# Twenty columns of experts by pairs instead of sixteen, with a third buffer, splits on GpSimd and separate memory for the last stage

## The chip, the cores and the metric

The kernel runs on one core of a Trainium2 chip. The metric is the device time of one execution in microseconds; of the kernel before there are three runs. A core has five engines with a queue of their own each, and every queue is worked off in order: TensorE (PE: matmuls; PEld: the load of the stationary operand), VectorE (DVE), ScalarE (ACT), GpSimd (POOL) and SyncE (SP). SP and ACT start plain transfers, POOL plain and indexed ones; the transfers themselves run on 16 DMA engines.

## The reference

One encoder layer over 256 tokens of 2048 features. Behind the mixing part (pooling and latent attention) stands PEER, a retrieval over 128 x 128 = 16384 experts of one neuron each:

```python
h = h + jnp.concatenate([y_pool, y_mla], axis=-1) @ w_out[i]
h = h + peer(rms_norm(h, ffn_norm_gain[i]), w_pq[i], sub_k1[i], sub_k2[i], expert_u[i], expert_v[i])
gate = jax.nn.sigmoid(rms_norm(h, ple_norm_gain[i]) @ w_ple_gate[i])
h = h + gate * (p[i] @ w_ple_proj[i])

# in peer: 8 heads pick 16 of 128 x 128 experts for every token, with softmax gates
act = jax.nn.gelu(jnp.einsum('tkd,td->tk', expert_u[ib], xb))
return jnp.einsum('tk,tkd->td', act * gb, expert_v[ib])
```

So each token has 128 expert slots. For a slot the dot product of the token with the expert's row of U is taken, its gelu is multiplied by the gate, and with that coefficient the expert's row of V is added. All of it is in f32.

## The kernel before

**Columns.** The 16384 experts stand as 128 columns of 128. For a dense column the kernel computes all 256 tokens against all 128 experts: the U tile of the column (1 MB) comes in two halves of 128 x 1024, each is split into two fp32r parts (`hi` on ACT, `lo` = value - `hi` on DVE, L108 and L110), and 48 matmuls of 256 columns follow (L220 to L222, three for each of 16 slices). ND = 112 columns go this way, one after the other.

**Pairs.** The other NP = 16 columns (104 to 119) are computed only where a token picked an expert: the pairs (token, expert) are listed in chunks of up to four of one token, 128 chunks to a set, NS = 9 sets (NCH = 8 chunks for a token at most). A *step* takes one of the four pairs of each of 128 chunks and one half of the features: an indexed transfer `ur<-in_UP` brings 128 half rows of U (512 KB), and one DVE instruction (L1106) multiplies them with the tokens' half rows `xr` (512 KB, loaded for every fourth step) and sums. There are 9 x 2 x 4 = 72 steps. After a set its four columns of sums are scattered to `hidD` by indexed transfers (L1119). The `ur` and `xr` buffers are rings of two each; the gather of step k + 2 is issued when step k has been computed.

**The pairs' last stage.** When all sums are in `hidD`, four quarters q of 64 tokens follow (`pair_load_coefs`, `pair_coefs`): POOL loads the sums (L1129) and the gates (L1130) of a quarter into the two `ur` buffers, ACT takes the gelu, DVE multiplies (L1144) and takes the largest magnitude, and POOL writes the coefficients to `coefD` (L1147).

**Groups and lists.** In between, the gates are laid out for the dense columns by small matmuls with one-hot matrices, in 64 *groups* of four tokens (L1015). From the columns that are done, lists of used experts are built in three stages (columns 0 to 79, 80 to 119, 120 to 127: `classes`, `totals`, `ranks`, `places`, then `columns`, L1329 on PE). The list of the first stage names the first 17 tiles of V rows, that of the second needs the pairs' coefficients: its rank matmuls (L1254) wait for them.

**V tiles.** A V tile gathers 128 rows of V (`vraw`, 1 MB, L1382) and their coefficients (`cr`, L1395), splits both, and adds their product. The first eleven stand between the dense columns from column START = 100 on, two halves behind each; the other 86 run at the end, then the gated last matmul.

**What sets the order.** The loop over columns calls `u_hook` twice per column (once more in a V tile). Each call adds to a pace; while it is 1 or more, one task of the queue `side` (selection, groups, lists) is written into the program, and a second pace does the same for the queue `lq` of pair tasks (PAIR_PACE: 0.45 for each call while groups run, 1.0 afterwards). A scheduler then orders PE, ACT, DVE and POOL by times that it estimates; SP keeps the written order. `Feed` (L58 on) loads halves five ahead and splits two ahead; `hi` and `lo` have three buffers each. Splits whose number stands in `on_pool` get their `lo` part on POOL; before, those are two halves of V, none of U.

## Time and profile before

| | |
|---|---|
| median of 3 runs | 1674.48 us (1673.2 to 1678.94) |
| the profiled execution | 1681.48 us, span of its instructions 1679.8 us |
| PE | 1573.0 us busy (94%), 10548 matmuls |
| DVE | 1245.6 us (74%) |
| ACT | 887.8 us (53%) |
| POOL | 470.6 us (28%) |
| DMA | 396.24 MB, mean 236 GB/s |
| mean granted TensorE clock | 0.969 of full speed |

The shares are means over stages with different limits, so the stages are read apart: up to 387 us the layer's first part, then the dense columns to about 1219 us, the rest of the V tiles to 1568 us, and the last matmul. A busy PE counts pipelined matmuls, and one that runs at half clock is as busy as one at full clock; the time of a column is the better measure.

### The profile page before, as it was taken

The page shows a single profiled execution, that of the slowest core. Times are in us where ns is not written, and L with a number is a line of the kernel's source. Part 1 is how long each engine was busy: PE and PEld are TensorE (multiplying, and loading weights), DVE is VectorE, ACT ScalarE, POOL GpSimd, SP SyncE. Part 2 cuts the span into 40 slices and gives each one's busy share as a digit, 9 for nine tenths or more (in the row PEclk, how much of TensorE's full clock was granted, in tenths as well). Part 3 has the DMA queues.
Part 4 walks back from the last instruction along what each step waited for, and adds up shares of the span by engine and source line. Part 5 has one row for each costly group of instructions (what it writes and reads, how often), then busy time and mean ns, then how long its engine had stood idle before and what let it go on. Part 6 is the DMA issues. An engine that isn't in the chain of part 4 may idle for free. (4 is left out here: it accounts for less than half of the span.)

```text
span 1679.8 us, 27995 instructions
## 1 busy us (share of the span) xinstructions
PE 1573.0 (94%) x10548; PEld 1424.9 (85%) x10548; DVE 1245.6 (74%) x2233; ACT 887.8 (53%) x1615; POOL 470.6 (28%) x396
## 2 busy tenths in 40 slices
PE   8999999999999999999899889673989999999997
PEld 6888787999999899999898789663877888888886
DVE  5575658899997688888796779463886667667764
ACT  6765445544543577777533333241456556556653
POOL 0010000000000323232432354431247776676000
PEclk9999999999999999999999999896999999999999
DMA  8663366556555576777799888675778888888263
GB/s 298 206 197 116 126 210 236 178 166 231 182 185 183 184 236 220 254 250 234 259 353 349 316 288 271 240 263 175 227 301 328 297 291 295 287 293 298 84 218 110
DMA packets 101252, 396.24 MB, mean 236 GB/s; under 512 B 14131, under 2 KB 19412, under 8 KB 85620
## 3 DMA queue, kind: packets, MB, share of 16 engines
q1 hardware_dynamic: 59908, 221.26, 39.4%
q0 software_dynamic: 34720, 168.00, 28.7%
q10 hardware_dynamic: 6480, 5.11, 0.9%
q8 instruction: 84, 1.38, 0.3%
q14 instruction: 60, 0.49, 0.1%
HBM read 367.01 MB, written 27.32 MB: 235 GB/s over the span
## 5 line engine op out<-in xcount | busy, mean ns | idle before, releaser
L108 ACT CAST hi<-raw 128x1024 fp32r<-128x1024 f32 (+2 forms) x382 | 392.4, 1029 | 457.6 <-PE bank L221 311.5
L110 DVE TENSOR_TENSOR lo<-raw,hi 128x1024 fp32r<-128x1024 f32 (+2 forms) x382 | 455.7, 1195 | 142.9 <-ACT hi L108 139.4
L222 PE MATMUL bank<-xnH,lo 128*128 128x256 f32 x1792 | 513.8, 288 | 15.7 <-DVE lo L110 15.7
L220 PE MATMUL bank<-xnH,hi 128*128 128x256 f32 x1792 | 520.4, 291 | 1.6 <-ACT hi L108 1.6
L221 PE MATMUL bank<-xnL,hi 128*128 128x256 f32 x1792 | 513.8, 287 | 0.0
L222 PEld LDWEIGHTS bank<-xnH,lo 128*128 128x128 f32 x1792 | 349.2, 196 | 17.2 <-DVE lo L110 16.7
L220 PEld LDWEIGHTS bank<-xnH,hi 128*128 128x128 f32 x1792 | 350.6, 196 | 2.6 <-ACT hi L108 2.0
L221 PEld LDWEIGHTS bank<-xnL,hi 128*128 128x128 f32 x1792 | 350.6, 196 | 0.2
L110 DVE TENSOR_TENSOR lo<-vraw,hi 128x1024 fp32r<-128x1024 f32 x192 | 233.7, 1224 | 104.3 <-ACT hi L108 93.5
L108 ACT CAST hi<-vraw 128x1024 fp32r<-128x1024 f32 x194 | 203.1, 1048 | 103.7 <-PE bank L222 70.2
L221 PE MATMUL bank<-lo,ccH 128*128 128x512 f32 x520 | 208.0, 400 | 2.6 <-DVE lo L110 2.6
L222 PE MATMUL bank<-hi,ccL 128*128 128x512 f32 x520 | 207.2, 398 | 0.0
L220 PE MATMUL bank<-hi,ccH 128*128 128x512 f32 x520 | 156.8, 400 | 23.1 <-ACT hi L108 22.3
L1382 POOL DMA_INDIRECT vraw<-in_V,idx x97 | 129.0, 1330 | 124.2 <-DVE lo L110 49.6
L1099 POOL DMA_INDIRECT ur<-in_UP,uidx x72 | 94.9, 1319 | 243.0 <-DVE hp L1106 183.1
L1395 POOL DMA_INDIRECT cr<-coefD,idx x97 | 126.6, 1305 | 52.9 <-issue 27.2
L220 PEld LDWEIGHTS bank<-hi,ccH 128*128 128x128 f32 x520 | 98.1, 191 | 47.8 <-ACT hi L108 24.5
L221 PEld LDWEIGHTS bank<-lo,ccH 128*128 128x128 f32 x520 | 99.2, 191 | 27.0 <-DVE lo L110 4.1
L222 PEld LDWEIGHTS bank<-hi,ccL 128*128 128x128 f32 x520 | 99.2, 191 | 22.5
L1106 DVE CUSTOM_DVE_ANT_0 ur<-ur,xr 128x1024 f32<-128x1024 f32 x72 | 87.7, 1218 | 36.5 <-DMA ur<-in_UP,uidx 36.4
L233 ACT ACTIVATE oo<-oo,gT 128x128 bf16<-128x128 bf16 x256 | 81.8, 395 | 6.9 <-DVE oo L1004 6.8
L221 PE MATMUL bank<-hgL,hi 128*128 128x256 f32 x256 | 73.3, 287 | 4.0 <-DVE hgL L730 4.0
(401 smaller groups left out, 2380.2 us busy)
## 6 DMA issues: line engine op xcount, KB each, us to landing
raw<-in_U SPq DMA_DIRECT2D x224, 512.0 KB
raw<-in_w_out SPq DMA_DIRECT2D x32, 512.0 KB
raw<-in_w_pq SPq DMA_DIRECT2D x32, 512.0 KB
raw<-in_w_gate SPq DMA_DIRECT2D x32, 512.0 KB
raw<-in_w_in_p SPq DMA_DIRECT2D x16, 512.0 KB
...
```

The costliest lines, as they stand in the source:

```text
L108: self.nc.scalar.copy(hi[:, :w], r)
L110: eng.tensor_tensor(lo[:, :w], r, hi[:, :w].bitcast(F32), op=OP.subtract)
L220: pe.matmul(ps, ah, bh, start=start, stop=False)
L221: pe.matmul(ps, ah, bl, start=False, stop=False)
L222: pe.matmul(ps, al, bh, start=False, stop=stop)
L233: act.activation(dst, ps, AF.Copy, scale=scale)
L1099: pool.indirect_dma_start(out=u, out_offset=None, in_=a["UP"], in_offset=bass.IndirectOffsetOnAxis(ap=lst["uidx"][:, half, s, i:i + 1], ax ...
L1106: tc.keep_in_program_order(dve.tensor_tensor_reduce(out=u, in0=u, in1=lst["x"][s, half], scale=1.0, scalar=0.0, op0=OP.mult, op1=OP.add, a ...
L1382: pool.indirect_dma_start(out=raw, out_offset=None, in_=a["V"], in_offset=bass.IndirectOffsetOnAxis(ap=row(c, i, 0), axis=0))
L1395: pool.indirect_dma_start(out=cr[:, :w], out_offset=None, in_=src, in_offset=bass.IndirectOffsetOnAxis(ap=row(c, i, 1), axis=0))
```

## The change

NP becomes 20: four dense columns fewer (108), four more by pairs. NCH and NS become 10 and 11, which makes 88 steps of the 72. START becomes 96, the pairs' pace while groups run 0.6, the pace of `side` outside the groups 1.3. Rows of U get a third buffer, and `pair_loads(k + 2)` is issued ahead of step k instead of behind it. Of the halves of U tiles 26 to 97 every third has its `lo` part on POOL: `U_POOL` is a range of columns, 144 halves, and a V tile stands among them; POOL gets 49 of the splits. Behind the last step `pair_end` gives the pairs' memory back and opens new memory: two buffers for a quarter's sums, one each for gates and coefficients; between load and use of a quarter stand two empty tasks instead of one (four at the first). One DVE multiplication of the list stage (L1318) goes to ACT. Two empty tasks are put into a list stage, and the loop waits at column START for the first coefficients' loads to be written.

```diff
-NP = 16
+NP = 20
-NCH = 8
-NS = 9
+NCH = 10
+NS = 11
 BETWEEN = 11
-START = 100
-PAIR_PACE = (0.45, 1.0)
+START = 96
+PAIR_PACE = (0.6, 1.0)
+U_POOL = (26, 98)
...
+    first = next(u for u, x in enumerate(units) if x[0] is u_tiles[U_POOL[0]])
+    last = next(u for u, x in enumerate(units) if x[0] is u_tiles[U_POOL[1] - 1])
+    feed.on_pool = [n for n, (u, i) in enumerate(feed.parts) if first <= u <= last and n % 3 == 0]
...
-        u = lp.tile([P, ring_w], F32, name="ur", tag="ur", bufs=2)[:, :1024]
+        u = lp.tile([P, ring_w], F32, name="ur", tag="ur", bufs=3)[:, :1024]
...
         s, half, i = steps[k]
+        if k:
+            pair_loads(k + 2)
         u = lst["u"].pop(k)
...
-        pair_loads(k + 2)
...
+    def pair_end():
         while lst["out"]:
             pair_out()
+        close(cms["L"])
+        cms["L"], st["lp"] = open_pool(name="pairs2", side="right")
+        lst["mx"] = st["lp"].tile([P, NP], F32, name="mx")
+
+    def pair_load_coefs(q):
         lp = st["lp"]
         w = NP * 64
-        hq = lp.tile([P, ring_w], F32, name="ur", tag="ur", bufs=2)[:, :w]
-        gq = lp.tile([P, ring_w], F32, name="ur", tag="ur", bufs=2)[:, :w]
+        hq = lp.tile([P, w], F32, name="hq", tag="hq", bufs=2)
+        gq = lp.tile([P, w], F32, name="gq", tag="gq")
...
-        cq = lp.tile([P, ring_w], F32, name="xr", tag="xr", bufs=2)[:, :NP * 64].rearrange("p (n t) -> p n t", t=64)
+        cq = lp.tile([P, NP, 64], F32, name="cq", tag="cq")
...
+        lq.append(pair_end)
         for q in range(4):
-            lq.extend([lambda q=q: pair_load_coefs(q), lambda: None, lambda q=q: pair_coefs(q)])
+            lq.append(lambda q=q: pair_load_coefs(q))
+            lq.extend([lambda: None] * (4 if q == 0 else 2))
+            lq.append(lambda q=q: pair_coefs(q))
...
-        dve.tensor_scalar(oh[:, 1], oh[:, 0], i2col, None, op0=OP.mult)
+        evac_scaled(oh[:, 1].rearrange("p k n -> p (k n)"), oh[:, 0].rearrange("p k n -> p (k n)"), i2col)
...
-        out = [lambda f=f: f(s) for f in (classes, totals, ranks, places, places2, places3)]
+        out = [lambda f=f: f(s) for f in (classes, nothing, totals, ranks, nothing, places, places2, places3)]
...
-        st["pace"] += 1.75 if st["wk"] and st["groups"] < 64 else 1.0
+        st["pace"] += 1.75 if st["wk"] and st["groups"] < 64 else 1.3
...
+            while j == START and not crs:
+                hook()
```

In the program, the groups stand between columns 23 and 58 (29 and 64 before), the last step of the pairs at column 90 (99), the last list matmul of the first stage in column 94 (99), the first V tile behind column 96 (100), and the rank matmuls of the second stage behind the sixth V tile in both.

POOL's queue where the pairs' steps run beside dense columns; before (a piece of the steps behind the groups; `hidD<-hp` is the scatter of sums):

```order
L1099 DMA ur<-in_UP,uidx 128x1024 x4
L1095 DMA xr<-xnD,rowx 128x1024
L1119 DMA hidD<-hp,hidx 528896x1
L1099 DMA ur<-in_UP,uidx 128x1024 x2
L1119 DMA hidD<-hp,hidx 528896x1
L1099 DMA ur<-in_UP,uidx 128x1024
L1119 DMA hidD<-hp,hidx 528896x1
L1099 DMA ur<-in_UP,uidx 128x1024
```

The same queue now, in the same part (L112 is the split's `lo` half, L1106 the gather of U rows, L1127 the scatter):

```order
L112 TENSOR_TENSOR lo<-raw,hi 128x1024
L1127 DMA hidD<-hp,keys 660992x1
L1106 DMA ur<-in_UP,uidx 128x1024 x2
L1102 DMA xr<-xnD,rowx 128x1024
L112 TENSOR_TENSOR lo<-raw,hi 128x1024
L1106 DMA ur<-in_UP,uidx 128x1024
L1127 DMA hidD<-hp,keys 660992x1
L112 TENSOR_TENSOR lo<-raw,hi 128x1024
L1106 DMA ur<-in_UP,uidx 128x1024 x2
```

Splits of U now stand between gathers and scatters, and each waits until those ahead of it in the queue have been issued.

POOL's queue in the pairs' last stage before, from the loads of quarter 0 to those of quarter 2 (`ur<-hidD` sums, `ur<-gateD` gates, `coefD<-xr` coefficients, `cr` and `vraw` of V tiles):

```order
L1129 DMA ur<-hidD 128x1024
L1130 DMA ur<-gateD 128x1024
L1395 DMA cr<-coefD,idx_11434 128x128
L1382 DMA vraw<-in_V,idx_11434 128x2048
L1147 DMA coefD<-xr 128x8x64 x2
L1129 DMA ur<-hidD 128x1024
L1130 DMA ur<-gateD 128x1024
L1395 DMA cr<-coefD,idx_11434 128x128
L1382 DMA vraw<-in_V,idx_11434 128x2048
L1395 DMA cr<-coefD,idx_11434 128x128
L1147 DMA coefD<-xr 128x8x64 x2
L1129 DMA ur<-hidD 128x1024
```

And now (L1142 loads sums, L1143 gates, L1160 writes coefficients, L1412 and L1399 are those of V tiles):

```order
L1142 DMA hq<-hidD 128x1280
L1143 DMA gq<-gateD 128x1280
L1142 DMA hq<-hidD 128x1280
L1412 DMA cr<-coefD,idx_11115 128x128
L1399 DMA vraw<-in_V,idx_11115 128x2048
L1412 DMA cr<-coefD,idx_11115 128x128
L1160 DMA coefD<-cq 128x8x64 x2
L1160 DMA coefD<-cq 128x4x64
L1143 DMA gq<-gateD 128x1280
L1142 DMA hq<-hidD 128x1280
```

The sums of the next quarter are loaded one quarter ahead; its gates still follow the coefficient writes, of which there are three instead of two.

## Rows read from the trace of the kernel before

**Rows 1.** Busy time of each engine by stretch of the span: from and to (us), length, then busy us and instructions of PE, PEld, DVE, ACT and POOL, the granted TensorE clock, the share of the DMA engines and GB/s.

```profile
387.00:520.00 133.00, 133.00 (x1111) 133.00 (x1110) 125.86 (x303) 62.98 (x79) 3.26 (x6) 1.00 0.61 198
520.00:556.00 36.00, 36.00 (x317) 35.87 (x316) 26.40 (x64) 15.72 (x23) 4.33 (x5) 1.00 0.58 188
556.00:567.00 11.00, 7.51 (x71) 6.89 (x70) 4.05 (x6) 4.00 (x10) 7.54 (x8) 0.96 0.36 113
567.00:818.00 251.00, 251.00 (x2420) 246.93 (x2418) 216.81 (x364) 189.53 (x571) 66.50 (x53) 0.99 0.73 237
818.00:1063.00 245.00, 220.60 (x1777) 218.26 (x1775) 198.65 (x328) 84.23 (x112) 95.24 (x75) 0.95 0.87 309
1063.00:1080.00 17.00, 6.82 (x52) 6.61 (x50) 3.71 (x15) 2.37 (x6) 9.13 (x11) 0.80 0.51 167
1080.00:1104.00 24.00, 22.20 (x132) 19.57 (x132) 12.64 (x13) 12.04 (x16) 12.18 (x11) 0.90 0.89 325
1104.00:1164.00 60.00, 24.95 (x135) 20.70 (x136) 29.73 (x37) 16.82 (x23) 17.50 (x20) 0.68 0.67 225
1264.00:1568.00 304.00, 303.20 (x1305) 245.35 (x1304) 208.91 (x233) 183.25 (x233) 201.01 (x149) 1.00 0.81 284
```

**Rows 2.** The same view of the instructions that use `xnH`, two of the three matmuls of each slice, so 32 of a column's 48; columns as above without POOL.

```profile
420.00:460.00 40.00, 40.00 (x224) 34.67 (x223) 0.00 (x0) 0.00 (x0) 1.00 0.57 181
600.00:700.00 100.00, 87.45 (x450) 71.58 (x450) 0.00 (x0) 0.00 (x0) 1.00 0.72 238
820.00:1060.00 240.00, 209.08 (x1102) 178.58 (x1101) 0.00 (x0) 0.00 (x0) 0.95 0.88 311
```

**Rows 3.** Groups of instructions in the stretch 818 to 1063 us: line, engine, operation, tiles, shapes, count | busy us, mean ns of one | idle time of the engine before them and what ended it.

```profile
L110 DVE TENSOR_TENSOR lo<-raw,hi 128x1024 fp32r<-128x1024 f32 x70 | 84.9, 1220 | 7.0 <-ACT hi L108 6.6 <-issue 0.3
L108 ACT CAST hi<-raw 128x1024 fp32r<-128x1024 f32 x70 | 73.4, 1049 | 137.9 <-PE bank L221 128.4 <-DVE lo L110 2.3 <-PE bank L222 2.0
L1099 POOL DMA_INDIRECT ur<-in_UP,uidx x40 | 53.4, 1336 | 99.5 <-DVE hp L1106 72.8 <-DVE oh L1319 9.2 <-DVE oh L1318 7.0
L1106 DVE CUSTOM_DVE_ANT_0 ur<-ur,xr 128x1024 f32<-128x1024 f32 x42 | 51.2, 1220 | 33.3 <-DMA ur<-in_UP,uidx 33.1
L1119 POOL DMA_INDIRECT hidD<-hp,hidx x21 | 28.8, 1372 | 47.4 <-DMA hidD<-hp,hidx 29.1 <-DVE hp L1112 15.3 <-issue 2.7
L1095 POOL DMA_INDIRECT xr<-xnD,rowx x9 | 9.8, 1088 | 2.7 <-issue 2.7
L1318 DVE TENSOR_SCALAR oh<-oh,i2col 128x392 bf16<-128x392 bf16 x20 | 6.1, 318 | 0.0
L1106 DVE DVE_READ_ACCUMULATOR2_ANT hp<- 128x1 f32 x42 | 3.4, 81 | 0.0
L1255 ACT CAST used<-bank 128x384 bf16<-128x384 f32 x1 | 0.5, 480 | 6.4 <-PE bank L1254 6.4
```

**Rows 4.** GB/s of the DMA engines in 40 equal slices of 818 to 1063 us.

```profile
GB/s 274 167 406 246 320 314 396 386 349 368 408 378 367 207 290 405 381 199 276 422 397 343 320 313 146 295 279 291 294 342 350 267 262 329 265 300 227 223 359 195
```

**Rows 5.** The instructions in order of time around the only two splits on POOL: start us, duration us, engine, line, operation, tiles, count [idle time before].

```profile
1232.67 0.17 DVE L1278 TENSOR_TENSOR cf<-cf,ok 128x8 f32<-128x8 f32 x1
...
1232.99 2.41 POOL L110 TENSOR_TENSOR lo<-vraw,hi 128x1024 fp32r<-128x1024 f32 x1
...
1233.35 2.08 DVE L1278 TENSOR_TENSOR used<-used,ok 128x8 f32<-128x8 f32 x1
...
1236.02 3.02 DVE L1298 TENSOR_TENSOR used<-used 128x8 f32<-128x8 f32 x1
...
1236.65 2.35 POOL L110 TENSOR_TENSOR lo<-vraw,hi 128x1024 fp32r<-128x1024 f32 x1
```

**Rows 6.** POOL in order of time in the pairs' last stage, columns as in rows 5.

```profile
1073.52 0.94 POOL L1382 DMA_INDIRECT vraw<-in_V,idx  x1 [0.30 <-issue]
...
1084.89 0.95 POOL L1382 DMA_INDIRECT vraw<-in_V,idx  x1 [0.30 <-issue]
...
1090.82 0.94 POOL L1382 DMA_INDIRECT vraw<-in_V,idx  x1 [1.93 <-DVE lo L110]
1093.48 0.60 POOL L1129 DMA_DIRECT2D ur<-hidD  x1 [1.72 <-DMA hidD<-hp,hidx]
1094.07 0.58 POOL L1130 DMA_DIRECT2D ur<-gateD  x1
...
1106.41 0.98 POOL L1147 DMA_DIRECT2D coefD<-xr  x1 [6.10 <-DVE xr L1144]
1109.73 0.93 POOL L1147 DMA_DIRECT2D coefD<-xr  x1 [2.34 <-issue]
1110.65 0.57 POOL L1129 DMA_DIRECT2D ur<-hidD  x1
```

**Rows 7.** DVE in order of time there: the product of each of the four quarters.

```profile
1104.57 1.23 DVE L1144 TENSOR_TENSOR xr<-ur 128x1024 f32<-128x1024 f32 x1 [5.50 <-DMA ur<-gateD]
...
1123.38 1.22 DVE L1144 TENSOR_TENSOR xr<-ur 128x1024 f32<-128x1024 f32 x1
...
1145.09 1.22 DVE L1144 TENSOR_TENSOR xr<-ur 128x1024 f32<-128x1024 f32 x1
...
1159.98 1.23 DVE L1144 TENSOR_TENSOR xr<-ur 128x1024 f32<-128x1024 f32 x1 [11.41 <-DMA ur<-gateD]
```

**Rows 8.** PE in order of time: the first matmul of the first V tile, and the longest waits behind it.

```profile
1080.29 1.22 PE L220 MATMUL bank<-hi,ccH 128*128 128x512 f32 x2 [10.47 <-ACT hi L108]
...
1141.46 1.22 PE L220 MATMUL bank<-hi,ccH 128*128 128x512 f32 x2 [9.32 <-ACT hi L108]
1163.57 0.29 PE L1254 MATMUL bank<-used 128*128 128x128 bf16 x1 [18.78 <-DVE used L1248]
```

More of the change, by code (lines that the diff above doesn't have):

```diff
@@ L181, in emit @@
     order = [(1, i) for i in range(EARLY)]
+    u_tiles = []
     for j in range(ND):
-        unit(a["U"][j])
+        u_tiles.append(a["U"][j])
+        unit(u_tiles[j])
         if START <= j < START + BETWEEN:
@@ L1029, in group @@
         st["groups"] += 1
-    ring_w = max(1024, NP * 64)
+    ring_w = 1024
     lq = deque()
@@ L1044, in pairs_index @@
         lst["uidx"] = lp.tile([P, 2, NS, 4], I32, name="uidx")
-        lst["hidx"] = lp.tile([P, NS, 4], I32, name="hidx")
+        lst["hidx"] = keys.bitcast(I32)
         lst["hp"] = lp.tile([P, 2, NS, 4], F32, name="hp")
@@ L1084, in pairs_index2 @@
         dve.tensor_tensor(lst["hidx"], adr, free, op=OP.add)
-        pair_loads(0)
-        pair_loads(1)
+        for k in range(3):
+            pair_loads(k)
     def pair_loads(k):
@@ L1120, in pair_out @@
             ap=lst["hidx"][:, s, c:c + 1], axis=0), in_=lst["hp"][:, 0, s, c:c + 1], in_offset=None)
-    def pair_load_coefs(q):
+    def pair_end():
         while lst["out"]:
             pair_out()
+        close(cms["L"])
+        cms["L"], st["lp"] = open_pool(name="pairs2", side="right")
+        lst["mx"] = st["lp"].tile([P, NP], F32, name="mx")
+    def pair_load_coefs(q):
         lp = st["lp"]
         w = NP * 64
-        hq = lp.tile([P, ring_w], F32, name="ur", tag="ur", bufs=2)[:, :w]
-        gq = lp.tile([P, ring_w], F32, name="ur", tag="ur", bufs=2)[:, :w]
+        hq = lp.tile([P, w], F32, name="hq", tag="hq", bufs=2)
+        gq = lp.tile([P, w], F32, name="gq", tag="gq")
         pool.dma_start(hq, hid_pairs[:, q * w:(q + 1) * w])
         pool.dma_start(gq, gateD.rearrange("p a n t -> p (a n t)")[:, q * w:(q + 1) * w])
-        lst["hg"] = hq, gq
+        lst[q] = hq, gq
     def pair_coefs(q):
@@ L1136, in pair_coefs @@
         lp = st["lp"]
-        hq, gq = lst["hg"]
-        cq = lp.tile([P, ring_w], F32, name="xr", tag="xr", bufs=2)[:, :NP * 64].rearrange("p (n t) -> p n t", t=64)
+        hq, gq = lst.pop(q)
+        cq = lp.tile([P, NP, 64], F32, name="cq", tag="cq")
         act.activation(hq, hq, AF.Gelu_apprx_tanh)
@@ L1152, in pair_coefs @@
         else:
-            mx = lst["hp"].rearrange("p a s c -> p (a s c)")[:, :NP]
+            mx = lst["mx"]
             dve.tensor_reduce(mx, cq, axis=AX.X, op=OP.max, apply_absolute_value=True)
@@ L1365, in stage_tasks @@
         lo, hi = STAGES[s:s + 2]
-        out = [lambda f=f: f(s) for f in (classes, totals, ranks, places, places2, places3)]
+        nothing = lambda s: None
+        out = [lambda f=f: f(s) for f in (classes, nothing, totals, ranks, nothing, places, places2, places3)]
         for k in range(lo, hi, 4):
```

## The prediction

> **What bounds the kernel now.** I read the busy time by stretch first, then the column pitch, the groups of the pairs' stretch with their waits, and last the time order of the stall behind the first V tile.
>
> A dense column costs 5.71 us where PE is never out of work: 224 matmuls of 32 per column are 7 columns in 40 us [rows 2]. Columns 0 to 28 run at that pace (387 to 556 us), with DVE busy 125.9 + 26.4 = 152 of 169 us [rows 1]. Columns 29 to 64 carry the groups: 450 / 32 = 14.1 columns in 100 us, 7.11 us each [rows 2], PE full and DVE busy 216.8 of 251 us [rows 1]. A gap of 3.5 us without PE work lies at 556 to 567 us [rows 1]; with the slow columns around it I count 7 us.
>
> Columns 65 to 99 (818 to 1063 us) have no groups, yet take 245 / 35 = 7.0 us: PE is busy 220.6 of 245 us, the clock is 0.95 [rows 1]. DVE stands 33.1 us before steps whose U rows have not landed; 42 steps run here, 1.2 a column, and the gather of step k + 2 waits for step k, 72.8 us of POOL's idle time [rows 3]. As DVE works in order, splits stand behind such a step, and PE behind the splits. DMA is not idle either: 309 GB/s in the mean [rows 1], about 400 in the best slices [rows 4].
>
> The largest hole follows. The first V tile starts at 1080.3 us after 10.5 us without work [rows 8]. Then the pairs' last stage: PE works 25 of the 60 us from 1104 to 1164 us at a mean clock of 0.68 [rows 1], waits 9.3 us for a split that is queued behind it and 18.8 us for the ranks [rows 8]. The quarters' products are 19, 22 and 15 us apart [rows 7], so a chain sets this stretch. The V tiles from 1264 us on are limited by PE (303.2 of 304 us at full clock [rows 1]), and the change doesn't touch them.
>
> **The change part by part.** All sums are against the profiled execution: 1681.5 us, of which 1679.8 us are the span.
>
> *Four columns.* 4 x 5.71 = 22.8 us of PE work go. This is certain so long as PE is what limits; below I count column by column, so it isn't added again.
>
> *Selection earlier.* The groups start at column 23, so DVE has the same selection work in six columns less. Of its 152 us in columns 0 to 28, 58 splits of 1.22 us (that of [rows 3]) are 71 us; 81 us are other work. Now it needs 46 x 1.22 + 81 = 137 us in 23 columns, where PE needs 131: 23 columns take about 138 us. Bounds: 131 (work slips behind column 23) and 143 (longer lists of keys, jitter).
>
> *Splits on POOL.* Two splits on POOL stand in the trace, 2.41 and 2.35 us long. While they run, DVE products of 8 columns with both inputs in SBUF, which elsewhere take 0.17 us, take 2.08 and 3.02 us and end within 0.04 us of the POOL split's end [rows 5]. So a split on POOL seems to hold up such DVE instructions, and nearly all that DVE does in these columns is of that kind (splits, steps, one-hots). Two thirds of a POOL split per column free DVE of 0.67 x 1.22 = 0.81 us and block it for up to 0.67 x 2.38 = 1.59 us. I take the whole block, since the two cases agree; the other bound is no block.
>
> The Trainium skill ("SBUF — State Buffer", section "Who interferes with whom") says that a DVE instruction with two SBUF inputs and a GpSimd instruction that reads SBUF exclude each other, whichever starts first. The trace agrees in one direction with the 2.08 and 3.02 us; that POOL also waits for DVE no row shows. By the rule a POOL split would come up to one DVE instruction later, which is part of the first rival.
>
> *Group columns (36).* DVE now has 216.8 / 251 x 7.11 = 6.14 us a column. Steps go from 0.9 to 1.2 a column (twice the pace): +0.3 x 1.30 = 0.39; the splits -0.81; the block +1.59: 7.31 us against PE's 7.11. So 36 x 0.2 = 7 us are lost; bounds 0 (no block) and 25 (POOL splits late by about 0.7 us a column, half of a gather of 1.34 us that stands ahead [rows 3]).
>
> *Columns 59 to 90, with steps.* By the order 51 steps run here in 32 columns, 1.6 a column. Per column: DVE 198.65 / 35 = 5.68, + 0.4 x 1.30 - 0.81 + 1.59 = 6.98 us (without the block 5.4). POOL: 1.6 gathers of 1.34, 0.4 loads of tokens of 1.09, 0.8 scatters of 1.37 us, two thirds of a split: 2.14 + 0.44 + 1.10 + 1.59 = 5.3 us, and 29.1 / 21 = 1.4 us of wait for the scatter before at each of 0.8 scatters: 6.4 us. DMA: 309 GB/s x 7.0 us = 2.16 MB now, + 0.4 x (0.52 + 0.13) = 2.42 MB, 6.05 us at 400 GB/s. PE 5.71 and some lists. The third buffer takes the gather's landing off the path: the gather goes out one step earlier, and most of the 33.1 us should go. But DVE, POOL and DMA now each need 6 to 7 us, in order, and wait for one another. I take 7.3 us a column, 234 us. Bounds: 6.5 (no block, gathers hidden; 208) and 8.3 (each POOL split held for a gather or scatter of 1.3 to 1.4 us and not absorbed; 266). The five columns behind take 6.0 us.
>
> *First V tile.* The list of stage 0 ends in column 94, two columns ahead of the first V tile; it was one. From the end of column 99 (1063 us) to the V tile it is 17 us now, of which one column is covered. With a column more and no scatter ahead of the first load, 10.5 us of wait shrink to 3. Bounds 0 and 10.
>
> Added up: 387 + 138 + 7 + 36 x 7.11 + 7 + 234 + 30 + 6 (column 96) + 3 = 1068 us for the start of the first V tile, 12 us earlier than now.
>
> *The last stage.* Both versions have six V tiles and some five columns, about 44 us of PE work, between the first V tile and the ranks. Now it is 1163.6 - 1080.3 = 83 us [rows 8]: 13 us until the loads of quarter 0, 11 until its product, 55 for the other three, 4 to the ranks [rows 6, 7]. After the change the loads of quarter 0 stand one V tile earlier in POOL's queue, behind the fourth (1084.9 instead of 1090.8 us [rows 6]): 6 us. In a quarter's turn the gelu leaves the path, as its sums are loaded ahead. The gates don't: they have one buffer, and their load stands behind three writes. From the end of a product to the next load it is 1110.65 - 1105.8 = 4.9 us for two writes; a third adds 0.93 + 2.34 = 3.3 us [rows 6]. With 8 us to land (1094.1 to 1104.6 is 10.4; that of the last quarter at most as long) a turn is 1.2 + 4.9 + 3.3 + 8 = 17.4 us, three are 52. Sum: 7 + 11 + 52 + 4 = 74 us, 9 us less. Bounds: 50 (the waits were V tiles in POOL's queue and go with it) and 95 (25% more data in a turn, all of it on the path).
>
> *Small edits.* L1318 moves 32 x 0.32 = 10 us from DVE to ACT, which has less to do; one costs ACT about 0.48 us, as the nearest copy [rows 3]. If ACT were late with it, lists would end 5 us later. Memory opened anew waits for the last step's readers, eight columns ahead. I count both at nothing.
>
> Behind the ranks both have seven columns, so the end moves with them: -12 - 9 = -21 us, and the profiled 1681.5 becomes about 1660; on the median of 1674.5 that is 1653 us. The stretch bounds add to -65 and +55 us, rarely together.
>
> **The rivals.**
>
> *POOL becomes the bound (slower).* Its queue is in order: a split behind a gather waits for DVE's step, a split behind a scatter for the scatter before (29.1 us of wait in 21 [rows 3]). PE gets a half two halves ahead, 5.7 us; `hi` 1.05 + `lo` 2.4 leave 2.2 us, and one gather and one wait are 1.34 + 1.4 = 2.7 us. From the point at which the mean hold of the 49 splits exceeds 2.2 us, each adds to PE. At a hold of 3.1 us it is 0.9 x 49 = 44 us above the sum's absorbed case, -21 + 44 = +23: 1697 us. Against it: before, POOL is busy just 95 of 245 us [rows 1], and PE's own waits slow the others down too.
>
> *The waits were the whole cost (much faster).* If DVE isn't blocked and the gathers are hidden, 32 columns take 208 us (-26), the groups lose nothing (-7), and the last stage shrinks to 55 us (-19): -73, about 1602 us. For it speaks that DVE waits 33 us for gathers alone, against it rows 5 and the 400 GB/s.
>
> *The change moves the wait only.* The chain of quarters takes its 83 us again, since a turn has more data; columns 59 to 90 take 7.6 us: -21 + 9 + 10, about 1672 us. This is no change.
>
> That the listed pairs overflow their larger lists, so that the slow branch for all experts runs, I exclude: counted from the reference's inputs, 1354 chunks of 1408 are needed, and at most 30 pairs of 40 for a token.
>
> **How the numbers follow.** The forecast (-10 to -45 us) gets 0.55, the much faster case 0.13, no gain 0.12, POOL as the bound 0.20. A measurement of this kernel tells 0.3%, 5 us, from no change. Faster: 0.13 + 0.55 + a small part of the third, 0.71; within 0.3%: 0.09; slower 0.20. The range of 1610 to 1695 leaves out the far half of the fast case and some of the slow one. Of the likeliest case alone it is 1630 to 1665 us.
>
> **What would show it.** Right: 108 columns; the first V tile near 1068 us; DVE products and splits of above 2 us beside POOL's splits of U; the idle time of DVE for `ur` well below 33 us; the rank wait of PE 10 us shorter, with quarters 17 us apart. Wrong: PE waits for `lo` from POOL of several us each (POOL is the bound), splits of 1.22 us on DVE beside those on POOL (no block), or quarters below 12 us apart.

## The result: slower by 0.9%

The changed kernel takes 1689.51 us (median of 4 runs, 1687.2 to 1691.11), the kernel before 1673.84 us on the same chip (4 runs). The ratio is 1.0088, with an interval of 1.0071 to 1.0104. Forecast were 1653 us and a gain. The profiled execution took 1691.1 us, of which 1689.3 us are the span of its instructions.

### The profile page after: what moved, and what is told of

It is laid out like the page before. It is cut to its first block, busy times and chain, and to the rows that moved or that the text cites. A ratio compares the mean times of both kernels' runs of the same rounds, so it can differ in the third digit from the quotient of the medians.

```text
span 1689.3 us, 27663 instructions
## 1 busy us (share of the span) xinstructions
PE 1566.3 (93%) x10360; PEld 1407.8 (83%) x10360; DVE 1289.1 (76%) x2184; ACT 895.7 (53%) x1638; POOL 631.6 (37%) x480
## 4 chain that ended last, share of the span: by engine, by line
PE 51%; DVE 15%; issue 7%; POOL 5%; DMA 3%; ACT 2%; DVEq 0%; POOLq 0%; ACTq 0%
PE bank L229 17%; PE bank L228 16%; PE bank L227 16%; DVE lo L112 4%; DVE ur L1115 2%; DVE oo L1009 2%; POOL lo L112 2%; DVE oo L1011 1%; DMA ur<-in_UP,uidx 1%; POOL ur L1106 1%; ACT hi L110 1%; DVE CA L1189 1%; PE bank L1022 1%; POOL keys L1055 1%; DMA gq<-gateD 1%
## 5 line engine op out<-in xcount | busy, mean ns | idle before, releaser
L229 PE MATMUL bank<-xnH,lo 128*128 128x256 f32 x1728 | 499.3, 290 | 26.5 <-POOL lo L112 16.1
L112 DVE TENSOR_TENSOR lo<-raw,hi 128x1024 fp32r<-128x1024 f32 (+2 forms) x325 | 396.4, 1222 | 148.8 <-ACT hi L110 146.3
L227 PE MATMUL bank<-xnH,hi 128*128 128x256 f32 x1728 | 503.8, 292 | 2.0 <-ACT hi L110 2.0
L228 PE MATMUL bank<-xnL,hi 128*128 128x256 f32 x1728 | 496.9, 288 | 0.0
L229 PEld LDWEIGHTS bank<-xnH,lo 128*128 128x128 f32 x1728 | 338.3, 196 | 31.0 <-POOL lo L112 18.4
L227 PEld LDWEIGHTS bank<-xnH,hi 128*128 128x128 f32 x1728 | 339.7, 197 | 3.4 <-ACT hi L110 2.2
L228 PEld LDWEIGHTS bank<-xnL,hi 128*128 128x128 f32 x1728 | 339.4, 196 | 0.3
L112 DVE TENSOR_TENSOR lo<-vraw,hi 128x1024 fp32r<-128x1024 f32 x192 | 237.2, 1243 | 98.4 <-ACT hi L110 98.3
L1399 POOL DMA_INDIRECT vraw<-in_V,idx x97 | 127.3, 1313 | 122.1 <-DVE ccL L237 39.5
L1106 POOL DMA_INDIRECT ur<-in_UP,uidx x88 | 121.2, 1377 | 125.8 <-DVE hp L1115 80.1
L1412 POOL DMA_INDIRECT cr<-coefD,idx x97 | 123.6, 1274 | 57.4 <-issue 29.6
L112 POOL TENSOR_TENSOR lo<-raw,hi 128x1024 fp32r<-128x1024 f32 x49 | 124.3, 2537 | 27.4 <-ACT hi L110 22.1
L1115 DVE CUSTOM_DVE_ANT_0 ur<-ur,xr 128x1024 f32<-128x1024 f32 x88 | 123.0, 1403 | 4.1 <-DMA ur<-in_UP,uidx 2.9
```

The costliest lines, as they stand in the source:

```text
L112: eng.tensor_tensor(lo[:, :w], r, hi[:, :w].bitcast(F32), op=OP.subtract)
L227: pe.matmul(ps, ah, bh, start=start, stop=False)
L228: pe.matmul(ps, ah, bl, start=False, stop=False)
L229: pe.matmul(ps, al, bh, start=False, stop=stop)
L1106: pool.indirect_dma_start(out=u, out_offset=None, in_=a["UP"], in_offset=bass.IndirectOffsetOnAxis(ap=lst["uidx"][:, half, s, i:i + 1], ax ...
L1115: tc.keep_in_program_order(dve.tensor_tensor_reduce(out=u, in0=u, in1=lst["x"][s, half], scale=1.0, scalar=0.0, op0=OP.mult, op1=OP.add, a ...
```

## The profile after

Busy time by stretch of the changed kernel: the stall behind column 20, the columns with groups (23 to 58), columns 59 to 95, the first V tiles, and the stretch up to the ranks (columns as in [rows 1]).

```profile
502.00:535.00 33.00, 22.24 (x183) 21.64 (x181) 29.29 (x88) 9.02 (x16) 5.98 (x6) 0.79 0.34 105
535.00:816.00 281.00, 266.14 (x2495) 256.47 (x2493) 255.31 (x370) 191.84 (x579) 166.93 (x110) 0.99 0.76 254
816.00:1082.00 266.00, 235.23 (x1874) 230.82 (x1874) 219.87 (x305) 100.61 (x141) 167.36 (x112) 0.95 0.85 303
1082.00:1131.00 49.00, 38.66 (x236) 34.51 (x236) 28.70 (x28) 21.21 (x29) 28.53 (x27) 0.86 0.82 288
1131.00:1172.00 41.00, 15.20 (x76) 11.25 (x75) 22.01 (x29) 11.02 (x14) 15.10 (x16) 0.69 0.79 284
```

Against the prediction's sum, stretch by stretch:

| stretch | forecast | after |
|---|---|---|
| columns 0 to 22 | 138 | 148 |
| columns 23 to 58, with groups (36 x 7.11, 7 for the gap ahead of them, 7 for the splits) | 270 | 281 |
| columns 59 to 95 | 264 | 265 |
| column 96 and the wait for the first V tile | 9 | 8 |
| first V tile to the ranks | 74 | 82.5 |

The differences are +10, +11, +1, -1 and +8.5, together +29.5 us. Behind the ranks nothing changed: 516 us from there to the end before, 517 us after. This accounts for the profiled executions, of which one of 1660 us was forecast and one of 1691 us measured. Between the medians, 1653 and 1689.5 us, it is 36.5 us, because the profiled execution of the kernel before lies 7 us above its median and that of the changed kernel only 1.6 us.

What PE waited for in 500 to 1240 us (what it waited for: us in total, times, longest us):

```profile
PE bank L1270 <- DVE used L1264: 22.0, 1, 22.0
PE bank L229 <- POOL lo L112: 16.1, 10, 2.9
PE bank L1345 <- DVE oh L1335: 11.8, 5, 8.6
PE bank L227 <- ACT hi L110: 10.5, 5, 4.7
```

The wait for the ranks is the longest single one, as before (18.8 us, [rows 8]). Ten waits for a split from POOL are new. The stall behind column 20 is two waits of PE (in order of time):

```profile
513.31 0.47 PE L923 MATMUL bank<-ident,e 128*128 128x128 f32 x1 [4.66 <-DVE e L825]
...
520.31 0.16 PE L871 MATMUL bank<-nbf,triones 128*128 128x2 bf16 x1 [6.10 <-DVE nbf L863]
```

PE's queue is in order: the small matmuls of the selection stand ahead of dense columns in it and wait for DVE, which has no room there (29.3 of 33 us busy); the granted clock is 0.79 there.

A split on POOL and the DVE instruction beside it, in the group columns:

```profile
674.97 3.81 DVE L1115 CUSTOM_DVE_ANT_0 ur<-ur,xr 128x1024 f32<-128x1024 f32 x1
...
675.33 2.36 POOL L112 TENSOR_TENSOR lo<-raw,hi 128x1024 fp32r<-128x1024 f32 x1
```

The step takes 3.81 us instead of the usual 1.22. What this comes to is seen in the groups of 535 to 816 us (count | busy us, mean ns | idle before):

```profile
L1009 DVE TENSOR_TENSOR oo<-iotas,eT 128x1024 bf16<-128x1024 bf16 x62 | 65.3, 1053 | 4.0 <-PE bank L1022 4.0
L112 DVE TENSOR_TENSOR lo<-raw,hi 128x1024 fp32r<-128x1024 f32 x49 | 62.3, 1270 | 5.6 <-ACT hi L110 5.5
L112 POOL TENSOR_TENSOR lo<-raw,hi 128x1024 fp32r<-128x1024 f32 x23 | 59.8, 2602 | 20.9 <-ACT hi L110 16.3 <-ACT CA L1185 4.2
L1115 DVE CUSTOM_DVE_ANT_0 ur<-ur,xr 128x1024 f32<-128x1024 f32 x41 | 57.2, 1397 | 2.2 <-DMA ur<-in_UP,uidx 1.1 <-DMA xr<-xnD,rowx 1.1
L1011 DVE TENSOR_TENSOR oo<-oo,gT 128x1024 bf16<-128x1024 bf16 x62 | 54.0, 872 | 0.6
```

A split can also be late. PE's waits in the same stretch, and one of the four for POOL with what stands ahead of it in POOL's queue: a scatter that waits until the one before has landed, then the split.

```profile
PE bank L229 <- POOL lo L112: 8.3, 4, 2.6
PE bank L1022 <- DVE oo L1011: 4.7, 6, 2.0
```

```profile
721.96 1.18 POOL L1127 DMA_INDIRECT hidD<-hp,keys  x1 [1.74 <-DMA hidD<-hp,keys]
723.17 2.72 POOL L112 TENSOR_TENSOR lo<-raw,hi 128x1024 fp32r<-128x1024 f32 x1
...
725.94 0.39 PE L229 MATMUL bank<-xnH,lo 128*128 128x256 f32 x1 [2.36 <-POOL lo L112]
```

In 816 to 1082 us DVE's idle time for gathered rows is 1.8 us (33.1 before, [rows 3]), but a step now takes 1408 ns (1220):

```profile
L1115 DVE CUSTOM_DVE_ANT_0 ur<-ur,xr 128x1024 f32<-128x1024 f32 x47 | 65.8, 1408 | 1.8 <-DMA ur<-in_UP,uidx 1.8
...
L112 POOL TENSOR_TENSOR lo<-raw,hi 128x1024 fp32r<-128x1024 f32 x24 | 59.7, 2488 | 6.4 <-ACT hi L110 5.9
```

The third buffer alone does not explain the 1.8 us: the run e1 below has it too, without splits on POOL, and there DVE waits 22.8 us for gathered rows in the same columns (799 to 1073 us):

```profile
DVE ur L1115 <- DMA ur<-in_UP,uidx: 22.8, 13, 4.3
```

The pairs' last stage on POOL, and DVE's products of the quarters with what stands ahead of them:

```profile
1096.84 1.01 POOL L1127 DMA_INDIRECT hidD<-hp,keys  x1 [0.30 <-issue]
...
1101.44 0.61 POOL L1142 DMA_DIRECT2D hq<-hidD  x1
1102.03 0.59 POOL L1143 DMA_DIRECT2D gq<-gateD  x1
...
1118.90 0.97 POOL L1160 DMA_DIRECT2D coefD<-cq  x1 [1.08 <-DVE cq L1157]
1122.57 1.68 POOL L1160 DMA_DIRECT2D coefD<-cq  x2 [2.69 <-issue]
1124.24 0.55 POOL L1143 DMA_DIRECT2D gq<-gateD  x1
```

```profile
1115.78 1.22 DVE L112 TENSOR_TENSOR lo<-vraw,hi 128x1024 fp32r<-128x1024 f32 x1
1116.92 1.48 DVE L1157 TENSOR_TENSOR cq<-hq,gq 128x1280 f32<-128x1280 f32 x1
...
1134.22 1.21 DVE L112 TENSOR_TENSOR lo<-vraw,hi 128x1024 fp32r<-128x1024 f32 x1
1135.35 1.48 DVE L1157 TENSOR_TENSOR cq<-hq,gq 128x1280 f32<-128x1280 f32 x1
...
1152.25 1.49 DVE L1157 TENSOR_TENSOR cq<-hq,gq 128x1280 f32<-128x1280 f32 x1
...
1167.84 1.49 DVE L1157 TENSOR_TENSOR cq<-hq,gq 128x1280 f32<-128x1280 f32 x1 [12.59 <-DMA gq<-gateD]
```

The first three products have no wait of their own: they follow directly behind splits (the first two of V tiles, the third of a half of U). Only the last waits for its gates.

## The experiments

A ratio is to the kernel before, run on the same chip in the same session. The medians of the kernel before lie between 1673.8 and 1682.1 us in the sessions, so ratios are compared, and differences of some tenths of a per cent across sessions prove little. "Rank wait" is PE's in both list stages together; times are of the profiled execution. The expectations call e1 the first run, e3 the third.

| run | ratio (interval) | last step | last product | first V tile | ranks | rank wait |
|---|---|---|---|---|---|---|
| before | 1 | 1057.1 | 1160.0 | 1080.3 | 1163.6 | 22.3 |
| after | 1.0088 (1.0071 to 1.0104) | 1048.4 | 1167.8 | 1089.4 | 1172.0 | 22.0 |
| e1 | 0.9890 (0.9867 to 0.9912) | 1011.3 | 1108.6 | 1091.8 | 1138.8 | 1.3 |
| e2 | 1.0323 (1.0299 to 1.0348) | 1104.9 | 1200.3 | 1095.3 | 1204.5 | 66.3 |
| e3 | 0.9992 (0.9976 to 1.0007) | 1043.4 | 1148.9 | 1059.9 | 1153.0 | 36.0 |
| e4 | 1.0096 (1.0074 to 1.0118) | 1098.0 | 1172.1 | 1076.0 | 1175.7 | 60.4 |
| e5 | 1.0165 (1.0143 to 1.0186) | 1066.8 | 1184.1 | 1091.7 | 1188.2 | 37.7 |
| e6 | 1.0090 (1.0070 to 1.0110) | 1058.4 | 1170.0 | 1075.7 | 1174.1 | 46.1 |
| e8 | 0.9950 (0.9934 to 0.9966) | 1025.6 | 1119.7 | 1102.5 | 1149.9 | none |
| e9 | 1.0037 (1.0020 to 1.0053) | 1053.5 | 1165.2 | 1075.8 | 1169.3 | 34.5 |
| e10 | 1.0033 (1.0018 to 1.0047) | 1047.5 | 1165.3 | 1088.4 | 1169.5 | 20.9 |
| e11 | 0.9960 (0.9939 to 0.9981) | 1046.9 | 1148.3 | 1063.0 | 1152.4 | 37.5 |
| e13 | 1.0070 (1.0046 to 1.0095) | 1084.4 | 1175.0 | 1114.7 | 1179.1 | 7.9 |
| e12 | 0.9881 (0.9829 to 0.9932) | 1000.7 | 1071.9 | 1112.6 | 1149.4 | 0.2 |
| e14 | 0.9927 (0.9903 to 0.9952) | 1005.5 | 1098.2 | 1092.2 | 1138.5 | 3.8 |
| e15 | 0.9917 (0.9896 to 0.9939) | 1006.4 | 1084.8 | 1099.7 | 1138.7 | 3.8 |
| e16 | 0.9924 (0.9902 to 0.9947) | 1044.2 | 1160.1 | 1060.5 | 1164.2 | 29.4 |
| e17 | 0.9963 (0.9935 to 0.9990) | 993.0 | 1066.2 | 1117.9 | 1154.7 | 5.1 |
| e20 | 0.9910 (0.9894 to 0.9926) | 1027.1 | 1112.9 | 1096.4 | 1142.5 | 1.9 |
| e18 | 0.9875 (0.9857 to 0.9893) | 994.8 | 1069.0 | 1094.6 | 1133.6 | 0.6 |

**Splits on POOL, and the selection's pace (e1 to e4).** e1 is the change without the splits on POOL:

```diff
-    feed.on_pool = [n for n, (u, i) in enumerate(feed.parts) if first <= u <= last and n % 3 == 0]
+    feed.on_pool = []
```

> The changed kernel with every lo part of U on DVE again. Theory 1 (a split on POOL blocks DVE for its whole length, and DVE then sets the group columns): no DVE product or step above 2 us beside the groups, the 36 group columns back from 281 us to 256-262 us, DVE busy there about 6.6 us a column, total 1655-1670 us. Theory 2 (the faster pair steps beside the groups cost the time): the group columns stay at 275 us or more, total 1685-1700 us.

Measured: 1656.83 us, in the range of theory 1, with 264 us for the group columns (256 to 262 expected). e2 is the change with the selection at the old pace (behind the groups 1.5 instead of 1.3, so that the lists still end in time), e3 both edits:

```diff
-        st["pace"] += 1.75 if st["wk"] and st["groups"] < 64 else 1.3
+        st["pace"] += 1.75 if st["wk"] and st["groups"] < 64 else (1.5 if st["groups"] == 64 else 1.0)
```

> The changed kernel with the selection at its old pace of 1.0 until the groups start (1.5 behind the groups, so that the lists are in time). Theory 1 (DVE cannot do the selection in 20 columns, and PE loses 15 us behind column 20): the stall of 502 to 535 us shrinks from 15 us to under 5, total 1675-1682 us. Rival (the same DVE work only moves, and what is won there is lost later because groups and lists run later): total 1686-1695 us.

> Both undone together. If the two costs are separate they add: 1640-1660 us. If one only hides the other: no less than the better of the two runs before, 1660-1680 us.

Measured: 1728.73 and 1674.15 us; the second is in the range of "one only hides the other", and above e1. e4 is the kernel before, with every third half of U tiles 26 to 97 split on POOL:

> The kernel before with every third half of U tiles 26 to 97 split on POOL and nothing else of the change. Theory 1 (the block): group columns 0.5 to 0.8 us longer each, total 1690-1705 us. Theory 2 (POOL's splits relieve DVE): DVE less busy beside the groups, total 1655-1675 us.

Measured: 1692.62 us. So the splits cost 2.0% on the change (1.0088 against 0.9890) and 1.0% on the kernel before. That e4 lies in the range of theory 1 is luck: its columns 29 to 64 grew by 6 us in all (269 for 263 us), 0.2 us each and not 0.5 to 0.8, although DVE was 20 us busier there (242 for 222 us). In its trace the ranks come 12 us later, and about half of that lies behind these columns, where the last step comes 41 us later and PE waits 60.4 us for the ranks instead of 22.3. e2 was a miss for both theories: the old pace costs 39 us instead of saving the stall. It takes the stall away (column 23 starts at 519.9 instead of 535.0 us), but all steps come later, and PE then waits 62 us for the ranks of the second stage.

The same groups in the group columns of e1 (535 to 799 us) say where the splits' time goes:

```profile
L112 DVE TENSOR_TENSOR lo<-raw,hi 128x1024 fp32r<-128x1024 f32 x72 | 87.9, 1221 | 5.6 <-ACT hi L110 5.0 <-issue 0.3
...
L1115 DVE CUSTOM_DVE_ANT_0 ur<-ur,xr 128x1024 f32<-128x1024 f32 x41 | 49.8, 1219 | 5.6 <-DMA xr<-xnD,rowx 3.5 <-DMA ur<-in_UP,uidx 2.1
...
L1009 DVE TENSOR_TENSOR oo<-iotas,eT 128x1024 bf16<-128x1024 bf16 x62 | 42.6, 687 | 5.0 <-PE bank L1022 5.0
L1011 DVE TENSOR_TENSOR oo<-oo,gT 128x1024 bf16<-128x1024 bf16 x62 | 42.6, 687 | 0.3
```

Without the splits the one-hots take 687 ns each, with them 1053 and 872: 62 x 0.366 + 62 x 0.185 = 34 us; the steps add 41 x 0.178 = 7 us, DVE's own splits 49 x 0.049 = 2 us. Three small products of the groups (`CA<-gl,CA`), 0.3 to 0.4 us long in e1, take 2.3 to 2.6 us here, which is 6 us more. That is some 50 us of DVE time lost beside 23 splits that free it of 23 x 1.22 = 28 us, a net loss of 22 us. The group columns are longer by 17 us (281 for 264 us), so a part of it was absorbed. How much of the 17 us comes through DVE and how much through late splits isn't separated: PE's waits for `lo` from POOL, of which e1 has none, are 8.3 us.

**Where on POOL (e8, e9).** `U_POOL` is (26, 59), the group columns alone, and (59, 98), those behind them.

> The changed kernel with splits on POOL only for columns 26 to 58, where the groups run (22 of the 49). Against the first run (none on POOL, 1656.8 us) the changed kernel lost 17 us in the group columns (281 us for 264), took 9 us less in columns 59 to 95 (265 for 274) and 24 us more from column 96 to the last column (146 for 122). Theory 1 in its narrow form (a split on POOL holds up DVE there and then): the group columns take 281 us again, the stretches behind them 274 and 122 us as in the first run: 1670 to 1678 us. Rival (the loss in the last stage comes from being late out of the groups): the last stage takes its 146 us here as well: 1685 to 1692 us. Rival 2 (the groups' loss is absorbed later): 1654 to 1660 us.

> The changed kernel with splits on POOL only for columns 59 to 97, behind the groups (27 of the 49). Theory (these splits stand among gathers and scatters in POOL's queue and push the loads of quarter 0 back behind V tiles): the group columns take 264 us, columns 59 to 95 about 265 to 274, and the last stage about 146 us: 1668 to 1682 us. Rival (the last stage's loss comes from the groups): 1648 to 1660 us.

Measured: 1669.88 and 1683.97 us, the one just below its first range, the other just above. In e8 the group columns lose 13 us against e1 (column 59 at 812.6 instead of 798.9 us), and the last stage stays hidden. In e9 they lose 2 us, but the last step comes at 1053.5 instead of 1011.3 us, and PE waits 34.5 us for the ranks. So the two halves of the splits cost in two ways: the first lengthens the columns with groups, the second makes the pairs' steps late.

**What sets the ranks (e5, e6, e10, e11).** e5 and e6 scatter the sums to two buffers in turn, on the change and on e3:

```diff
-        pool.indirect_dma_start(out=hidD, out_offset=...
+        pool.indirect_dma_start(out=(hidD, hidE)[c % 2], out_offset=...
+        pool.dma_start(hr, hid_pairs2[:, q * w:(q + 1) * w])
+        dve.tensor_tensor(hq, hq, hr, op=OP.add)
```

> The changed kernel with its 44 scatters of sums alternating between two separate buffers (both are zeroed, both loaded, DVE adds them, 4 x about 1.5 us, 2.6 MB more of zeros). As it is, each scatter waits until the one before has landed; in the changed kernel nine of them stand behind the last step (1048.4 us) and the last one goes out at 1096.8 us, 4.6 us ahead of the first load of sums (1101.4 us). Theory 3 (this chain of scatters, made longer by eight through the change, sets when the pairs' last stage starts): with two chains of 22 the last scatter comes some 20 us or more earlier, the loads of quarter 0 too, and most of the 22.0 us for which PE waits for the ranks goes: 1664 to 1676 us. Rival (the loads of quarter 0 stand where they do because of splits and V tiles in POOL's queue, the scatters only fill the time): within 5 us of 1690 us. Rival 2 (the turns of the quarters set the ranks, and each now loads half as much again): 1690 to 1700 us.

> The third run (no splits on POOL, selection at the old pace) with the same two buffers for the scatters. That run reached column 96 at 1043.8 us, 29 us earlier than the first run (1072.7 us), but its first load of sums came at 1098.8 us instead of 1046.6 us and PE waited 36.0 us for the ranks; its last step was at 1043.4 us and its last scatter at 1092.0 us. Theory 3 (chain of scatters): the load comes 20 us or more earlier and at least half of the 36 us goes: 1644 to 1658 us. Rival (POOL's queue behind V tiles): within 5 us of 1674 us. Rival 2 (turns of the quarters, which load more): 1674 to 1685 us.

Measured: 1706.68 and 1694.1 us. The loads of quarter 0 did come earlier, by 12 and 18 us (1089.7 for 1101.4, 1081.2 for 1098.8), although the last step was later in both. But `hr` shares the memory of `cq`, so its next load stands behind the writes (1127.2 us in e5), the addition comes at 1141.3 us, and the first turn grew to 34.5 us (35.3 in e6). The second rival holds, with more than the price it named; what a start 12 us earlier alone is worth stays open.

e10 and e11 load the gates of the next quarter ahead of the writes of this one (`pair_load_coefs(q + 1)` stands ahead of the loop over `coefD`):

> The changed kernel with the gates of the next quarter loaded ahead of the three coefficient writes of this one (same loads, same writes, other order in POOL's queue). In the changed kernel the load of the gates follows the product by 7.3, 10.1 and 11.0 us, because the writes stand ahead; the products are 18.4, 16.9 and 15.6 us apart, and PE waits 22.0 us for the ranks. Theory 4 (the turns of the quarters set the ranks, as the run with two buffers of sums suggested): each turn shrinks by 5 us or more, together 15 to 22 us: 1668 to 1676 us. Rival (a turn is set by the V tiles' splits in DVE's queue and by the transfers, not by the place of the load): 1684 to 1692 us.

> The third run (no splits on POOL, selection at the old pace; 1674 us, 36.0 us of waiting for the ranks) with the gates loaded ahead of the writes. There the gates' loads follow the products by 9.5, 8.9 and 7.2 us. Theory 4: three turns shrink by 5 us or more each, and the wait for the ranks with them: 1652 to 1660 us. Rival (a turn is set elsewhere): 1669 to 1678 us.

Measured: 0.55% below the change (9 us, of 15 to 22 expected) and 0.32% below e3 (5 us, of 14 to 22), the second with intervals that overlap; the times themselves, 1687.74 and 1675.42 us, lie in the rivals' ranges. In the traces the ranks come only 2.5 and 0.6 us earlier. The gates' load went out right behind the product (1117.30 instead of 1124.24 us), yet the products are 18.5, 16.9 and 14.4 us apart. On POOL of e10, and the last product on DVE:

```profile
1152.63 0.57 POOL L1143 DMA_DIRECT2D gq<-gateD  x1 [0.87 <-DVE cq L1157]
1153.22 0.95 POOL L1162 DMA_DIRECT2D coefD<-cq  x1
1161.31 1.66 POOL L1162 DMA_DIRECT2D coefD<-cq  x2 [7.14 <-issue]
```

```profile
1165.35 1.49 DVE L1157 TENSOR_TENSOR cq<-hq,gq 128x1280 f32<-128x1280 f32 x1 [11.49 <-DMA coefD<-cq]
```

So the first turns don't hang on the gates: their products stand where they are in DVE's order, behind splits. The last one now waits for the writes of the quarter before, since `cq` too has one buffer.

**The third buffer and the four columns (e13, e12).** e13 is e1 with two buffers and the gather behind the step again; e12 is e13 with NP = 16, NCH = 8, NS = 9, START = 100.

> The first run (changed kernel without splits on POOL, 1656.8 us) with two buffers for rows of U and the gather behind the step again, as in the kernel before. Theory 5 (the third buffer takes the gathers' landing off DVE's path, which cost 33.1 us of idle DVE in columns 65 to 99 before): the columns with steps grow by 10 to 25 us in all: 1667 to 1682 us. Rival (DVE waits for something else instead, since DMA and POOL are as busy as before): 1653 to 1661 us.

> The run with two buffers, and sixteen columns by pairs instead of twenty (9 sets instead of 11, 72 steps, first V tile behind column 100, 112 dense columns). With sixteen columns the third buffer doesn't fit into the memory, so this comparison is made with two. Theory 6 (the four columns are worth the time that PE needs for them where nothing else limits, 4 x 5.71 us): 15 to 25 us above the run with two buffers and twenty. Rival (the longer chain of 88 steps, 44 scatters and larger quarters takes it back): within 6 us of that run, or below it.

Measured: the third buffer, with the earlier gather, is worth 1.8% (1.0070 against 0.9890), more than expected: DVE waits 64.1 us for gathered rows in e13 and 24.9 us in e1 (535 to 1240 us):

```profile
DVE ur L1113 <- DMA ur<-in_UP,uidx: 64.1, 28, 7.2
```

```profile
DVE ur L1115 <- DMA ur<-in_UP,uidx: 24.9, 14, 4.3
```

And sixteen columns are 1.9% *faster* than twenty with the same two buffers: the rival had "or below it", but neither theory had this size. PE of e13 at the first V tile and at the ranks, and of e12 at the ranks:

```profile
1114.66 0.79 PE L227 MATMUL bank<-hi,ccH 128*128 128x512 f32 x1 [19.83 <-ACT hi L110]
...
1179.08 0.29 PE L1269 MATMUL bank<-used 128*128 128x128 bf16 x1 [7.89 <-DVE used L1263]
```

```profile
1149.43 0.23 PE L1269 MATMUL bank<-used 128*128 128x128 bf16 x1
```

In e12 the last product is at 1071.9 us, ahead of the first V tile, and PE comes to the ranks with 0.2 us of wait; in e13 it is 103 us later, among the V tiles.

**A later selection, later ranks, the paces alone (e14 to e17).** e14 is e12 with the paces of e3, e15 is e14 with the list multiplication back on DVE, e16 is e3 with `out[1:1] = [lambda: None] * 8` in the second list stage, e17 is the kernel before with PAIR_PACE (0.6, 1.0) and the pace 1.3.

> The run with sixteen columns and two buffers (0.988 of the kernel before), with the selection at the old pace (1.0 instead of 1.3; 1.5 behind the groups). In that run the last step is at 1000.7 us, the quarters' products run from 1026.0 to 1071.9 us beside dense columns, the first V tile starts at 1112.6 us and PE comes to the ranks at 1149.4 us with 0.2 us of wait: the chain has some 70 us to spare. Theory 7 (what counts is that this chain is hidden; the early selection only makes PE stall behind column 20, 15 us): a selection six columns later keeps the chain hidden and takes the stall away: 0.975 to 0.983. Rival (the early selection is what gives the gain): 0.993 to 1.003.

> As the run before it, and the list multiplication back on DVE. In the run with sixteen columns PE waits 25.0 us for one-hots of the lists (8.8 us in the kernel before) and DVE waits 10.7 us for the multiplication on ACT. Theory 8 (ACT is late with it, behind its hi parts): 4 to 15 us less than the run before it. Rival (the one-hots are late for other reasons, or DVE's own 10 us cost the same): within 4 us of it.

> The third run (twenty columns, no splits on POOL, selection at the old pace; 0.999 of the kernel before, PE waits 36.0 us for the ranks) with eight empty tasks ahead of the second stage's totals and ranks, so that PE has about three more columns with V tiles to do before it comes to them. Theory (PE stands at the ranks only because they come too early in its queue): 12 to 25 us less: 0.984 to 0.992. Rival (DVE, which waits for the same gates, holds up the splits as well, so PE then waits for splits): within 6 us of the third run: 0.995 to 1.003.

> The kernel before with the new paces alone (pairs 0.6 while groups run, side queue 1.3 outside them); memory, buffers, columns and lists as before. If the paces alone hide the quarters' chain, as theory 7 has it for sixteen columns: 0.983 to 0.992. Rival (the last stage's own memory and the sums loaded ahead give the gain; with the paces alone the stall behind column 20 costs 15 us): 1.000 to 1.010.

Measured: e14 0.9927, between both expectations, at the rival's edge. The stall behind column 20 is gone, but no gain over e12 shows. e15 0.9917: no difference by the place of the multiplication can be told. e16 0.9924: 0.7% below e3; the ranks stand two columns further back, but the products moved back as well (the last from 1148.9 to 1160.1 us), so PE still waits 29.4 us and the gain stays just short of the 12 to 25 us expected. e17 0.9963, between both expectations: the paces alone gain 0.4%, though they bring the stall behind column 20. The last step is 64 us earlier there (993.0 for 1057.1 us), and the rank wait 5.1 us.

**A pace between (e20, e18).** e20 is e1, e18 is e12, both with 1.15 for the selection and the list multiplication on DVE.

> The first run (twenty columns, three buffers, no splits on POOL; 0.989 of the kernel before) with the selection's pace at 1.15 instead of 1.3 and the list multiplication back on DVE. If PE's stall behind column 20 is DVE's backlog and the quarters' chain stays ahead of the first V tile (in the first run PE comes to the ranks at 1138.8 us with 1.3 us of wait, the last product is at 1108.6 us, so some 25 us are to spare and three columns later costs 18): 0.979 to 0.986. Rival (the chain, later by three columns, makes PE wait for the ranks again): 0.990 to 0.999.

> Sixteen columns, two buffers, no splits on POOL, the selection's pace at 1.15 and the list multiplication on DVE. Its neighbours on both sides (pace 1.3: 0.988; pace 1.0: 0.992 to 0.993) differ little, since the stall behind column 20 is replaced by waits at the end of the pairs. If a pace between them has neither: 0.978 to 0.986. Rival (what is taken away in one place comes back in another): 0.987 to 0.994.

Measured: 1660.6 and 1653.2 us. Both lie in the rivals' ranges, e20 not by its rival's mechanism: PE waits 1.9 us for the ranks, and most for the lists' one-hots (25.9 us). e18 has the lowest ratio of all, 1.25% below the kernel before; its interval overlaps those of e1 and e12. What PE waits for in it (387 to 1240 us):

```profile
PE bank L1344 <- DVE oh L1334: 23.1, 4, 9.0
PE bank L229 <- DVE lo L112: 16.5, 12, 2.9
PE bank L227 <- ACT hi L110: 6.0, 5, 3.1
```

The lists' one-hots are now the largest.

## Why the prediction was wrong

The range of 1610 to 1695 us holds the 1689.5 us, but the sign is wrong, and the likeliest case (1630 to 1665 us) missed.

- **The splits on POOL were mis-sized in the group columns; this step failed.** The sum gave them 7 us there, measured are 17 (281 us, 264 in e1). The block of DVE was foreseen, per split at its full length; measured were 50 us beside 59.8 us of splits. DVE's work wasn't set too low (7.31 us a column forecast, 255.3 / 36 = 7.09 measured), yet the columns took 7.81 us. What failed is the comparison of "7.31 us against PE's 7.11": the larger of two engines' sums was taken for the time, and the waits between the two queues were put at nothing, among them PE's 8.3 us for late splits, which stood only in the bound of 25 us. The bounds held the loss.
- **What the splits do to the last stage was left out.** They make the pairs' last step 37 us later than in e1 (1048.4 for 1011.3 us). In e1 three of the four quarters' products stand ahead of the first V tile and PE doesn't wait for the second stage's ranks at all: from the first V tile to the ranks it takes 47 us, below the bound of 50. In the changed kernel PE waits 22.0 us for them, and the stretch takes 82.5 us. In all the splits cost 2.0%. That e1 (1656.8 us) comes near the forecast is in part luck: it has the stall of the selection too, and a last stage that is hidden, of which the sum had neither.
- **The selection was mis-sized by 10 us**, 148 for 138 us, outside its bound of 143. DVE's work was summed against PE's again; that PE's queue holds small matmuls that wait for DVE ahead of dense columns was left out. Two such waits, 4.66 and 6.10 us, come to this size. The 7 us that the sum had for a gap ahead of the groups make up for a part by luck: the changed kernel shows no such gap.
- **"This is certain so long as PE is what limits"** (four columns, 22.8 us; not a term of the sum) failed in its condition. The last step came only 8.7 us earlier, and between it and the ranks lie 123.6 us instead of 106.5. With two buffers the four columns cost 1.9%; twenty columns with the third buffer are no gain over e12 (0.9890 against 0.9881). That a third buffer doesn't fit beside sixteen is said in the expectation of e12; no run shows it.
- **The last stage was mis-sized by 8.5 us.** The turn was right (17.4 us forecast, 17.0 in the mean), but its reason only for the last: the two others are set by places in DVE's order. The start was wrong: the loads of quarter 0 went out 12 us behind the first V tile (7 forecast), and the product came 15.5 us behind them (11), though its sums and gates had landed 11 and 6.7 us ahead of it and nothing but the order of ACT and DVE held it.
- **Columns 59 to 95 were right as a number** (265 for 264 us), which doesn't show their terms. The sum had the splits make them longer; without splits they took 274 us in e1, with a part of the hidden last stage among them. The third buffer was counted on for most of the 33.1 us of waiting for gathers; without the splits 22.8 us of waiting are left. The first V tile's wait was right (4.7 for 3 us).
- **The rival "POOL becomes the bound"** came near in time (1697 us), and its mechanism is there in part: PE waited for `lo` from POOL ten times, 16.1 us in all, never longer than 2.9 us, against the 44 us that it named.
- **The bounds were added up wrongly**: the stretches' own bounds give -67 and +83 us, where -65 and +55 stand.

A POOL split and the DVE instructions beside it, in order of time:

```profile
862.22 1.22 DVE L1115 CUSTOM_DVE_ANT_0 ur<-ur,xr 128x1024 f32<-128x1024 f32 x1
...
862.46 3.21 POOL L112 TENSOR_TENSOR lo<-raw,hi 128x1024 fp32r<-128x1024 f32 x1 [1.88 <-ACT hi L110]
...
863.37 3.38 DVE L112 TENSOR_TENSOR lo<-raw,hi 128x1024 fp32r<-128x1024 f32 x1
```

Here POOL waits too: its split, usually 2.4 us, ends 2.2 us behind the end of the step that ran when it was issued, and the next DVE split ends 1.1 us behind POOL's. All eleven POOL splits of U that took more than 2.6 us end 2.2 to 2.3 us behind the DVE instruction that ran when they were issued. The Trainium skill ("SBUF — State Buffer", section "Who interferes with whom") lets a DVE instruction with two SBUF inputs and a GpSimd instruction that reads SBUF exclude each other, whichever starts first. The trace agrees in both directions, with these rows and with the 3.81 us of the step beside a split of 2.36 us.
